# A two-layer diffusion backbone in fp32: stores of normalised tokens issued by GpSimd, and three SwiGLU tiles begun on the first half's tokens

## The chip, the core and the metric

The kernel runs on one core of a Trainium2 chip. TensorE (PE) multiplies, VectorE (DVE), ScalarE (ACT) and GpSimd (POOL) do the elementwise work, and SyncE (SP) issues the DMAs. Each of these engines works through its own queue in order: an instruction that waits holds up everything queued behind it on that engine. The metric is the device time of one execution in microseconds.

## What is computed

Latent and context tokens, 256 of each with 1024 features, go through two layers. Cut to what matters here:

```python
for l in range(2):
    m_x = split(silu(c) @ w_ada[l] + b_ada[l], 9)        # shift, scale, gate: three of each; m_c likewise from c_ctx
    x = post_norm(x, 0.5 * m_x[2] * swiglu(modulate(x, m_x[0], m_x[1]), ffn1_wi[l], ffn1_wo[l]), ln_g[l, 0], ln_b[l, 0])
    # the same for ctx
    y_x, y_c = hybrid_mixer(modulate(x, m_x[3], m_x[4]), ...)   # attention, RWKV, neighbourhood attention
    x = post_norm(x, m_x[5] * y_x, ...)                  # ctx in layer 0 only
    x = post_norm(x, 0.5 * m_x[8] * swiglu(modulate(x, m_x[6], m_x[7]), ...), ...)

def swiglu(u, wi, wo):
    gate, up = split(u @ wi, 2)
    return (silu(gate) * up) @ wo                        # 1024 -> 2 x 2816 -> 1024
def post_norm(x, y, g, b): return layer_norm(ALPHA * x + y, g, b)
```

## The kernel before, in words

Features lie on partitions and tokens on columns. The 512 columns are two halves: latent tokens (0 to 255, the first half) and context tokens (256 to 511, the second half). A product in full precision is three passes: each operand is split into a rounded high part and the rest, by one ACT copy (`whi`, `uh`; lines 320 and 336) and one DVE subtraction (`wlo`, `ul`; lines 321 and 337), and `gemm` (lines 330 to 332) multiplies high by high, low by high and high by low.

`wload` (line 312) loads a weight tile of 128x1024 into `raw`, of which there are three buffers, and splits it into `whi` and `wlo`, of which there are two each. A caller can give other buffers to hold the split tile (`hold`, four pieces of 128x512).

A stage is a SwiGLU (`ffn`) or a mixer. At its end the two halves are normalised one after the other: `ln_stats` sums squares on PE, takes `pow` on POOL (line 428) and spreads the result with a transpose (`ps_bc`). `ln_norm` multiplies (line 440), modulates for the next stage (`modulate`: `u`, `uh`, `ul`), and, in a second loop, has POOL scale the tokens for the residual path (`xn`, line 447), which SP stores to DRAM (`xd<-xn`, line 450). `xn` has two buffers, so the third one waits until the first store has landed. The second half's normalisation runs while PE has only the first half's tokens to work on.

A SwiGLU has 22 tiles m, each with a gate and an up product (`ps_fg`, `ps_fu`; PSUM has six banks for them, three tiles). With two halves, `early` tiles are started on the first half's columns and then finished on the second's; the others take all 512 columns at once. `swiglu` (line 496 and on) makes `sg` from both products and splits it into `hh` and `hl`. Tile 0's weights are loaded ahead (`make_ready`); those of the other early tiles are held in buffers of `hh` and `hl`.

Beside this, the modulations of later stages are worked out in pieces (`ada_pieces`): a piece loads 128x1024 of `w_ada` (`araw`, two buffers, line 242) and adds it to an accumulator with two DVE instructions (lines 251 and 253). `bg_after(1)` takes one piece from the list and queues its DVE instructions behind the latest `wlo` (`self.lo`). There are 45 pieces in the two SwiGLUs of layer 0 and 36 in the first of layer 1; two are taken with each tile.

Three SwiGLUs have two halves: both of layer 0 and the first of layer 1. Five normalisations store with `xn` on POOL: the two of those SwiGLUs that end in a mixer, the one that ends in a SwiGLU, and the two mixers. The last mixer and the last SwiGLU have only the first half.

The mixer begins with four tiles of `w_in`; the weights of two of them are held in buffers called `wG`, and its next tile is split into `phi` and `plo`.

A framework places the instructions: it lays each engine's order down ahead of time from the order in which the program names them, their dependencies and its own estimate of times, and adds waits where a buffer's memory was used by something before.

Of the kernel before, what the change touches and what calls it, by code (L numbers as in the profile page):

```python
# [112 lines left out]
class Program:  # L113
# [320 lines left out]
    def ln_norm(self, l, ln, h, nxt, dst, bc, res=None):  # L434


        nc, z = self.nc, self.z
        for k in range(KD):
            with (self.tc.issue_after(res.ins) if res is not None and k >= 3 else nullcontext()):
                nc.vector.tensor_tensor(out=z[k][:, h], in0=z[k][:, h], in1=bc, op=ALU.mult)  # L440
                if nxt is not None:
                    self.modulate(k, h, z[k][:, h], *nxt)
        for k in range(KD):
            xn = self.tmp.tile([P, SEQ], F32, tag="xn", name="xn", bufs=2 if nxt is not None else 4)
            lg, lb = [self.lng[:, l, ln, i, k:k + 1] for i in range(2)]
            if nxt is not None:
                nc.gpsimd.tensor_scalar(out=xn, in0=z[k][:, h], scalar1=lg, scalar2=lb, op0=ALU.mult, op1=ALU.add)
            else:
                nc.scalar.activation(out=xn, in_=z[k][:, h], func=AF.Identity, scale=lg, bias=lb)
            nc.sync.dma_start(out=dst[k][:, h], in_=xn)  # L450

    def norm_dst(self, l, ln, nxt, final=None):
        if nxt is not None:
# [8 lines left out]
    def ffn(self, l, which, halves, nxt_fn, every, final=None, then=()):  # L462
        nc = self.nc
# [4 lines left out]
        with ExitStack() as ctx:  # L468
# [7 lines left out]
            two = len(halves) == 2  # L476
            slots = iter(range(2 * KF))

            def load(m, held=False):
                ws = []  # L480
                for i in range(2):
                    hold = None
                    if held and m > 0:
                        hold = [[hp.tile([P, NT], F32R, tag=t, name="w" + t) for t in ("hh", "hl")] for _ in range(2)]
                    ws.append(self.wload(wi[m, i], 1024, hold=hold))
                    if next(slots) % every == 0:
                        self.bg_after(1)
                return ws

            def wi_gemm(ps, ws, h):  # L490
                for p, w in zip(ps, ws):
                    self.gemm(p[:, h], w, [t[:, h] for t in self.uh], [t[:, h] for t in self.ul])

            def swiglu(pg, pu):
                sg = self.tmp.tile([P, NT], F32, tag="sg", name="sg")
                nc.scalar.activation(out=sg[:, full], in_=pg[:, full], func=AF.Silu)
                nc.vector.tensor_tensor(out=sg[:, full], in0=pu[:, full], in1=sg[:, full], op=ALU.mult)
                a = hp.tile([P, NT], F32R, tag="hh", name="hh")
                b = hp.tile([P, NT], F32R, tag="hl", name="hl")
                self.split(a[:, full], b[:, full], sg[:, full])  # L500
                hh.append(a)
                hl.append(b)

            def banks():
                return [self.bank("mm", [P, NT], n) for n in ("ps_fg", "ps_fu")]


            early = 2 if two else 0
            ps = [banks() for _ in range(early)]
            ready, self.ready = self.ready, []  # L510
            ws = [m == 0 and ready or load(m, True) for m in range(early)]
            for h in halves if two else []:
                for m in range(early):
                    wi_gemm(ps[m], ws[m], h)
                    if h.start:
                        self.bg_after(1)
            for p in ps:
                swiglu(*p)
            for m in range(early, KF):
                p = banks()  # L520
                wi_gemm(p, m == 0 and ready or load(m), full)
                swiglu(*p)
                if self.bgpe:
                    self.bgpe.pop(0)()
            self.bg_all()
            gate = self.gate(l, gi)
            nxt = nxt_fn()
            dst = self.norm_dst(l, ln, nxt, final)
# [1126 lines left out]
```

## Time and profile before

| | |
|---|---|
| runs, us | 2874.34, 2883.58, 2884.24 |
| median, us | 2883.58 |
| profiled execution, us (its span) | 2877.69 (2875.9) |
| PE busy | 2706.8 us, 94% |
| DVE, ACT, POOL busy | 59%, 39%, 8% |
| mean granted TensorE clock | 0.963 |

"Busy" counts instructions at work. The timeline lists an engine's instructions in order of time, with what they waited for; the table of stretches shows the busy time of each engine between two points and the granted clock of TensorE.

### The profile page before, as it was taken

The numbers are of one execution on the slowest core, as the hardware profiler recorded it, in microseconds if no ns is written. First come the engines' busy times: TensorE is split into PE (matmuls) and PEld (weight loads), VectorE is DVE, ScalarE is ACT, GpSimd is POOL, SyncE is SP. The second block draws the span as 40 slices with busy tenths as digits, with TensorE's granted clock in tenths as the row PEclk, the third lists the DMA queues.
The fourth block names the chain that finished last, engine by engine and source line by source line (L and its number), as shares of the span: only waits on it lengthen the run. The fifth ranks groups of instructions, "written<-read, shape, count | busy, mean of one in ns | idle before, by whom it ended". The sixth has DMA issues, their size and how long they took to land. (4 is left out here: it accounts for less than half of the span.)

```text
span 2875.9 us, 48513 instructions
## 1 busy us (share of the span) xinstructions
PE 2706.8 (94%) x19654; PEld 2202.5 (77%) x19654; DVE 1704.9 (59%) x2855; ACT 1123.3 (39%) x2088; POOL 224.0 (8%) x242
## 2 busy tenths in 40 slices
PE   7999998999899899999999999999899998898998
PEld 5778887676667676787888878888877777777998
DVE  5667345767652457657762477533578775385654
ACT  3222235534432346342222332222565543373543
POOL 0000011000000101220000110001200000122000
PEclk9999998999999999999999999999999989898999
DMA  7655342321223533435553465433342223544654
GB/s 283 205 184 174 106 127 92 86 61 52 57 82 122 156 112 91 141 128 189 178 167 107 125 202 182 140 99 113 121 117 72 70 63 96 167 132 137 221 175 152
DMA packets 207616, 379.75 MB, mean 132 GB/s; under 512 B 80032, under 2 KB 110368, under 8 KB 207392
## 3 DMA queue, kind: packets, MB, share of 16 engines
q1 hardware_dynamic: 207392, 376.65, 42.2%
q8 instruction: 154, 2.52, 0.4%
q14 instruction: 70, 0.57, 0.1%
HBM read 342.50 MB, written 33.03 MB: 131 GB/s over the span
## 5 line engine op out<-in xcount | busy, mean ns | idle before, releaser
L320 ACT ACTIVATE whi<-raw 128x1024 fp32r<-128x1024 f32 (+1 forms) x399 | 415.2, 1041 | 1097.0 <-PE ps_o L331 297.3
L321 DVE TENSOR_TENSOR wlo<-raw,whi 128x1024 fp32r<-128x1024 f32 (+1 forms) x399 | 499.4, 1252 | 497.8 <-ACT whi L320 485.9
L847 PE MATMUL ps_gate<-uh,whi 128*128 128x512 f32 (+1 forms) x672 | 268.0, 399 | 4.6 <-ACT fg L853 3.3
L330 PE MATMUL ps_o<-hh,whi 128*128 128x512 f32 (+1 forms) x770 | 268.8, 349 | 0.0
L253 DVE SCALAR_TENSOR_TENSOR acc<-araw,cs,acc 128x1024 f32<-128x1024 f32 x210 | 260.5, 1279 | 13.6 <-DMA araw<-in_w_ada 13.0
L332 PE MATMUL ps_o<-hh,wlo 128*128 128x512 f32 (+1 forms) x770 | 267.9, 348 | 0.0
L331 PE MATMUL ps_o<-hl,whi 128*128 128x512 f32 (+1 forms) x770 | 266.6, 346 | 0.0
L330 PE MATMUL ps_fg<-uh,whi 128*128 128x512 f32 (+1 forms) x704 | 256.5, 364 | 7.6 <-ACT uh L336 3.8
L332 PE MATMUL ps_fg<-uh,wlo 128*128 128x512 f32 (+1 forms) x704 | 254.5, 361 | 6.7 <-DVE wlo L321 6.7
L332 PE MATMUL ps_fu<-uh,wlo 128*128 128x512 f32 (+1 forms) x704 | 251.9, 358 | 4.7 <-DVE wlo L321 4.7
L331 PE MATMUL ps_fg<-ul,whi 128*128 128x512 f32 (+1 forms) x704 | 253.6, 360 | 0.1
L330 PE MATMUL ps_fu<-uh,whi 128*128 128x512 f32 (+1 forms) x704 | 251.2, 357 | 0.9 <-ACT whi L320 0.9
L331 PE MATMUL ps_fu<-ul,whi 128*128 128x512 f32 (+1 forms) x704 | 250.9, 356 | 0.0
L849 PE MATMUL ps_gate<-uh,wlo 128*128 128x512 f32 (+1 forms) x672 | 243.8, 363 | 1.3 <-DVE wlo L321 1.3
L848 PE MATMUL ps_gate<-ul,whi 128*128 128x512 f32 (+1 forms) x672 | 243.6, 362 | 0.0
L330 PEld LDWEIGHTS ps_fg<-uh,whi 128*128 128x128 f32 x704 | 135.3, 192 | 39.1 <-ACT whi L320 12.0
L847 PEld LDWEIGHTS ps_gate<-uh,whi 128*128 128x128 f32 x672 | 132.4, 197 | 36.7 <-issue 7.2
L330 PEld LDWEIGHTS ps_o<-hh,whi 128*128 128x128 f32 x770 | 144.7, 188 | 20.4 <-ACT whi L320 1.7
L331 PEld LDWEIGHTS ps_o<-hl,whi 128*128 128x128 f32 x770 | 144.5, 188 | 20.1
L332 PEld LDWEIGHTS ps_o<-hh,wlo 128*128 128x128 f32 x770 | 144.7, 188 | 18.2
L332 PEld LDWEIGHTS ps_fg<-uh,wlo 128*128 128x128 f32 x704 | 135.1, 192 | 27.7 <-DVE wlo L321 8.2
L332 PEld LDWEIGHTS ps_fu<-uh,wlo 128*128 128x128 f32 x704 | 133.7, 190 | 26.1 <-DVE wlo L321 7.4
(299 smaller groups left out, 5099.4 us busy)
## 6 DMA issues: line engine op xcount, KB each, us to landing
raw<-in_ffn_wi SPq DMA_DIRECT2D x176, 512.0 KB, 3.6
araw<-in_w_ada SPq DMA_DIRECT2D x144, 512.0 KB, 3.8
raw<-in_w_in SPq DMA_DIRECT2D x92, 512.0 KB, 3.6
raw<-in_ffn_wo SPq DMA_DIRECT2D x70, 448.0 KB, 3.3
raw<-in_ffn_wo SPq DMA_DIRECT2D x35, 512.0 KB, 3.5
pd<-fg SPq DMA_DIRECT2D x52, 256.0 KB, 2.1
raw<-in_w_branch SPq DMA_DIRECT2D x24, 512.0 KB, 4.0
raw<-in_w_in SPq DMA_DIRECT2D x44, 256.0 KB, 2.7
```

The lines of the kernel that those rows point to most:

```text
L253: nc.vector.scalar_tensor_tensor(out=a, in0=raw, scalar=c, in1=a, op0=ALU.mult, op1=ALU.add)
L320: nc.scalar.activation(out=hi[:, :m], in_=r, func=AF.Copy)
L321: self.lo = nc.vector.tensor_tensor(out=lo[:, :m], in0=r, in1=hi[:, :m].bitcast(F32), op=ALU.subtract)
L330: nc.tensor.matmul(pt, wh, xh[k], start=first and k == 0, stop=False)
L331: nc.tensor.matmul(pt, wh, xl[k], start=False, stop=False)
L332: nc.tensor.matmul(pt, wl, xh[k], start=False, stop=last and k == n - 1)
L847: nc.tensor.matmul(pt, wh, xh, start=k == 0, stop=False)
L848: nc.tensor.matmul(pt, wh, xl, start=False, stop=False)
L849: nc.tensor.matmul(pt, wl, xh, start=False, stop=k == KD - 1)
```

## The change

GpSimd instead of SP issues the store of `xn` wherever a next stage follows. In a SwiGLU with two halves three tiles instead of two begin on the first half. The pieces that were taken with the held weight tiles and with the second half's products are no longer taken there; two are taken behind each early tile's `swiglu`. So six pieces are named by the end of tile 2, as before, and two with each later tile, as before. Since `self.lo` is then the last split of tile 2, all six are queued behind that on DVE.

```diff
-            nc.sync.dma_start(out=dst[k][:, h], in_=xn)
+            (nc.sync if nxt is None else nc.gpsimd).dma_start(out=dst[k][:, h], in_=xn)
...
-                    if next(slots) % every == 0:
+                    if not held and next(slots) % every == 0:
                         self.bg_after(1)
...
-            early = 2 if two else 0
+            early = 3 if two else 0
             ps = [banks() for _ in range(early)]
             ready, self.ready = self.ready, []
             ws = [m == 0 and ready or load(m, True) for m in range(early)]
             for h in halves if two else []:
                 for m in range(early):
                     wi_gemm(ps[m], ws[m], h)
-                    if h.start:
-                        self.bg_after(1)
             for p in ps:
                 swiglu(*p)
+                self.bg_after(2)
```

## Rows read from the trace of the kernel before

**Rows 1.** Stretches, busy us (instructions) per engine, then granted clock, DMA share, GB/s

```profile
425.00:458.00 33.00, 24.11 (x140) 21.26 (x139) 18.32 (x46) 19.23 (x45) 11.24 (x15) 0.75 0.47 140
1240.00:1312.00 72.00, 65.58 (x414) 57.33 (x415) 50.46 (x82) 30.86 (x60) 14.21 (x19) 0.95 0.50 163
1312.00:1625.00 313.00, 313.00 (x1429) 255.98 (x1428) 174.26 (x186) 82.37 (x100) 13.62 (x12) 1.00 0.48 151
```

**Rows 2.** The store's line and its tile: ns min/median/max; landing; us

```profile
L447 POOL TENSOR_SCALAR xn<-z,c_lngb x72: 553/557/2562, 422.0 to 2667.1; 128x256 f32<-128x256 f32 x72
L450 SPq DMA_DIRECT2D xd<-xn x72: 319/320/1594, 422.6 to 2667.7; - x72
DMA to landing us min/median/max: 1.7/1.7/4.7
```

**Rows 3.** First mixer's start: timeline (start, us, instruction [idle before <-releaser]) and a stretch

```profile
427.21 1.22 DVE L321 TENSOR_TENSOR wlo<-raw,whi 128x1024 fp32r<-128x1024 f32 x1
431.88 0.36 SPq L602 DMA_DIRECT2D raw<-in_w_in  x1
435.62 0.63 ACT L336 ACTIVATE phi<-raw 128x512 fp32r<-128x512 f32 x1 [3.15 <-DMA raw<-in_w_in]
436.61 2.72 PE L424 MATMUL ps_ss<-ones,sq 128*128 128x1 f32 x12 [1.78 <-ACT sq L420]
441.68 1.09 POOL L447 TENSOR_SCALAR xn<-z,c_lngb 128x256 f32<-128x256 f32 x2 [1.37 <-DVE z L440]
455.89 1.67 ACT L320 ACTIVATE wG<-raw 128x512 fp32r<-128x512 f32 x3 [2.96 <-DMA xd<-xn]
456.57 0.58 PE L330 MATMUL ps_first<-uh,wG 128*128 128x256 f32 x1 [2.43 <-ACT wG L320]
436.60:439.30 2.70, 2.69 (x12) 2.63 (x12) 0.38 (x1) 0.57 (x2) 0.00 (x0) 0.50 0.27 97
```

**Rows 4.** Timeline, second mixer's start

```profile
2041.72 1.97 PE L424 MATMUL ps_ss<-ones,sq 128*128 128x1 f32 x12 [2.04 <-ACT sq L420]
2043.97 0.70 POOL L428 TENSOR_TENSOR rs<-rs,mhalf 128x2 f32<-128x2 f32 x1 [6.16 <-DVE rs L427]
2046.04 1.09 POOL L447 TENSOR_SCALAR xn<-z,c_lngb 128x256 f32<-128x256 f32 x2 [1.37 <-DVE z L440]
2058.71 1.67 ACT L320 ACTIVATE wG<-raw 128x512 fp32r<-128x512 f32 x3 [1.46 <-DVE sh L897]
```

**Rows 5.** Second SwiGLU's start: timeline, a stretch, SP's wait, the load's median landing

```profile
1261.06 1.09 ACT L351 ACTIVATE u<-z,mb,mg 128x256 f32<-128x256 f32 x2 [4.74 <-DVE z L440]
1261.19 1.09 POOL L447 TENSOR_SCALAR xn<-z,c_lngb 128x256 f32<-128x256 f32 x2 [1.11 <-DVE z L440]
1275.79 0.81 SPq L242 DMA_DIRECT2D araw<-in_w_ada  x2
SPq L242 <- DMA xd<-xn: 0.9, 2, 0.6
araw<-in_w_ada SPq DMA_DIRECT2D x144, 512.0 KB, 3.8
1286.45 5.05 DVE L253 SCALAR_TENSOR_TENSOR acc<-araw,cs,acc 128x1024 f32<-128x1024 f32 x4
1292.69 0.80 PE L332 MATMUL ps_fg<-uh,wlo 128*128 128x512 f32 x1 [4.06 <-DVE wlo L321]
1293.00:1301.00 8.00, 7.92 (x23) 5.87 (x22) 7.66 (x7) 0.51 (x1) 0.00 (x0) 0.66 0.74 244
```

**Rows 6.** Timeline of PE, third SwiGLU's start

```profile
1645.18 0.38 PE L330 MATMUL ps_fg<-uh,whi 128*128 128x256 f32 x1 [1.47 <-ACT uh L336]
1685.15 0.50 PE L332 MATMUL ps_fg<-uh,wlo 128*128 128x512 f32 x1 [1.16 <-DVE wlo L321]
```

**Rows 7.** Timeline, last SwiGLU's start

```profile
2658.10 1.09 POOL L447 TENSOR_SCALAR xn<-z,c_lngb 128x256 f32<-128x256 f32 x2 [1.37 <-DVE z L440]
2669.65 1.28 ACT L496 ACT_TABLE_LOAD   x1 [0.92 <-DVE wlo L321]
```

## The prediction, made before the changed kernel was run

> **What bounds the kernel now.** I read the table of stretches first, to see where PE isn't at work. Inside a SwiGLU it never stops: 313.00 us busy of 313. Where one stage hands over to the next it does: 24.11 of 33 us at the first mixer's start with a granted clock of 0.75, 65.58 of 72 around the second SwiGLU's [rows 1]. The change touches only these seams, so all that it can give or cost is there: the first SwiGLU's start, then five seams in which tokens are normalised and stored. Next I read PE's timeline in each seam for the waits, then the timeline of the engine that each wait names, then the queue of SP.
>
> At the mixers' starts PE waits for squares from ACT, 1.78 and 2.04 us [rows 3, 4]. ACT was held by `phi`, which waited 3.15 us for a weight load that SP issued at 431.88 [rows 3], behind stores that wait for POOL. A `raw` buffer had come free when `wlo` ended, 427.21 + 1.22 = 428.43 [rows 3]; so 3.4 us of the load's delay are SP's queue. Later PE waits 2.43 us for `wG`, and `wG` waits for the landing of the last store, since it takes over memory [rows 3].
>
> At the second SwiGLU's start PE stands 4.06 us for a `wlo` on which DVE comes late: modulation pieces stand ahead of it in DVE's queue [rows 5]. Those began late because their loads were issued only at 1275.79, behind the stores, and waited for the landing of a store too [rows 5]. At the third SwiGLU's start a wait of 1.47 us goes back to a weight load behind stores, and three more, of 1.16, 0.95 and 1.02 (the first is shown), are `wlo` behind pieces [rows 6].
>
> **Part 1, the stores.** 72 of 0.32 us leave SP, 23 us of issuing that no end depends on [rows 2]. What counts is that weight loads no longer stand behind stores that wait for POOL. The squares' waits go: 1.78 and 2.04. In the first, the twelve `ps_ss` matmuls behind it took 2.72 us at a granted clock of 0.50, the lower level; at the higher they take 1.36, so 1.4 more, and 0.6 at the second mixer, where the same twelve took 1.97 [rows 3, 4]. I count both, with zero as the other end, since the normalisation's own pause behind them stays and can lower the clock a little later. At the third SwiGLU I let 1.1 of the 1.47 go, three quarters, since the load's own landing stays; ends zero and all of it [rows 6].
>
> The price is on POOL. Call c what issuing one store costs it. The trace has no DMA from POOL, so I bound c by the shortest and the longest issue on SP, 0.32 and 1.59 us [rows 2]. A POOL instruction with two columns to work on takes 0.70 [rows 4]; that plus one issue of 0.32 is 1.0, which I take, because it is the row of POOL itself with the least work in it. Below zero c can't go: POOL issues nothing now. A pair of buffers then turns in the longer of 2 x (0.56 + c) and 0.56 + c + 1.7 (landing) [rows 2]: 3.26 us at c = 1.0, and eight stores take 3 x 3.26 + 2 x 1.56 + 1.7 = 14.6 us from the first `xn` to the last landing (11.2 at c = 0.32, 19.0 at 1.59). What they take now: 455.89 - 441.68 = 14.2 at the first mixer, 12.7 at the second, 14.6 at the second SwiGLU (1275.79 - 1261.19), and at most 11.6 at the last, whose table load at 2669.65 didn't wait for it any more [rows 3, 4, 5, 7]. Who waits for that: `wG` at both mixers (+0.4 and +1.9 on the path), and the first `sg` of a SwiGLU, with ACT's next `whi` behind it. At the last SwiGLU the table load ahead of `sg` moves from 2669.65 to 2658.10 + 14.6 = 2672.7 [rows 7], 3.0 us, and the next tile's `whi` behind it; PE has a tile of work left then, so the cost is between 0 and 3.0, and I take 2.0, nearer to the upper end because nothing else hides a late `whi`. Also queued on POOL behind a store is `pow` of the second half; at c = 1.0 the first half's eight stores end before it is due, so nothing.
>
> The page "DMA: Bandwidth & Descriptors" of the Trainium skill (section Latency and other measured facts) speaks against this part: first byte about 1 us from GpSimd and 0.6 from SP, because software writes the descriptors. By it each of four turns would be about 0.4 us longer, an estimate of 1.6 us more at both mixers and the last SwiGLU, some 5 us in all; no row here shows a store from GpSimd.
>
> **Part 2, the third tile.** No PE work is added: 48 matmuls on 256 columns twice, instead of 48 on 512. Its weights are split in eight pieces instead of four instructions, during the normalisation, where ACT idles 4.74 us ahead of the second half's `u` [rows 5]; uncovered it would be 0.6 us a SwiGLU. PE has no pause between the first half's two tiles and the second half's, so a third adds nothing there. What it buys is at tile 3: `whi` and `wlo` come free when tile 0 is done, with 10.5 us of PE work on tiles 1 and 2 still to go (96 matmuls of half the 0.22 us that one takes on average in the long stretch [rows 1]), so tile 3's splits can lie ahead of the pieces. At the very first SwiGLU both halves are ready and I count nothing.
>
> **Part 3, the pieces.** As many as before, in the same total; their loads still wait for the stores' landing (`araw` takes over memory of theirs, as SP's wait shows [rows 5]). So POOL's pace, not SP's queue, sets when they begin, about as now at c = 1.0. They no longer stand ahead of tile 3's `wlo`, but can stand ahead of tile 4's: the first piece lands at 1275.79 + 3.8 = 1279.6, and PE, which stood at 1288.6 near the start of a tile, gets to tile 4 about 10.5 us later, at 1299.1 [rows 5]; in these 19.5 us DVE has six `sg` and `hl` (half a `wlo` of 1.22 each, 3.7 [rows 3]), one `wlo` and pieces of 2.5 (half of 5.05 us for four instructions [rows 5]). Five fit, a sixth makes PE wait, and a seventh and eighth are named with tile 3. I leave 1.5 us of wait where 4.06 was: -2.6. The stretch behind that wait had the clock at 0.66 for 7.92 us of work [rows 5], so (1 - 0.66) x 7.92 = 2.7 us go with it, if the wait is short; a wait of 1.16 us at the third SwiGLU is followed by full clock. There I take half of the three waits' 3.1: -1.5. Ends: all of both gone, or none.
>
> **Sum**, in us: first mixer -1.8 - 1.4 + 0.4 = -2.8; second SwiGLU -2.6 - 2.7 = -5.3; third -1.1 - 1.5 = -2.6; second mixer -2.0 - 0.6 + 1.9 = -0.7; last SwiGLU +2.0; total -9.4. Against the profiled execution's 2877.69 us (its span is 2875.9) that is 2868; this execution lies 6 us below the median of 2883.58, and I forecast the median: 2874 us, 0.3% less.
>
> **The rivals.** (a) *POOL is cheap and the waits vanish.* c near 0.32: the landing comes 3.0 and 1.5 us sooner at the mixers, the last SwiGLU loses nothing, pieces begin 3.4 us sooner and no `wlo` waits: -6.2, -4.1, -6.8, -4.2, 0 = -21, so 2862. For it: every wait goes back to SP's queue or the stores. Against: POOL's `pow` on two columns alone takes 0.70. 27 in 100.
>
> (b) *The wait only moves.* Pieces that begin at 1280 or later stand ahead of tile 4's `wlo` as they now do ahead of tile 3's, at the same cost; with the rest of the sum -2.8 - 1.1 - 0.7 + 2.0 = -2.6, so 2881. For it: the number of pieces by tile 2 is the same, and their loads stay bound to the landing. 20 in 100.
>
> (c) *Stores from POOL are slow.* c at 1.59: the stores take 19.0 us. `wG` comes 4.8 and 6.3 us later, `sg` of the last SwiGLU 7.4 with a wait of 6; `pow` of the second half stands behind the first half's stores (8 x 2.15 = 17 us) by 1 to 2 us at four seams, 5 in all; the SwiGLUs give nothing. So -5.8 of squares and clock, -1.1, + 4.8 + 6.3 + 6 + 5 = +15, and with the pieces later too up to +25: near 2900. It decides from c of about 1.5. 13 in 100. The page "SBUF — State Buffer" of the Trainium skill (section SBUF: two separate sides) has a mechanism for it: DVE instructions that take both SBUF ports lock GpSimd out of writing descriptors; no run so far shows it.
>
> **How the numbers follow.** The forecast has 40 in 100, (a) 27, (b) 20, (c) 13. A measurement of this kernel can tell about 0.5%, 14 us, from no change: below 2869 is (a), 0.27; within, the forecast and (b), 0.60; above, (c), 0.13. The range takes in (b), nearly all of (a) and half of (c): 2857 to 2899.
>
> **What would show it.** Right: a store issue on POOL near 1.0 us; no wait for `sq` behind `phi` at either mixer; the wait for `wG` still there and released by the store; DVE with tile 3's `wlo` ahead of the pieces. Wrong: PE waits of over 3 us at tile 4, POOL's `pow` late, or stores that land over 16 us after the first `xn`.

## The result, and the profile of the changed kernel

The changed kernel takes 2895.4 us (median of 6 runs, 2890.3 to 2898.8); the kernel before, run beside it, 2876.1 us (6 runs, 2871.6 to 2884.2). The ratio is 1.0057, with a 95% interval of 1.0043 to 1.0072: **the change makes the kernel 0.6% slower**, by some 16 to 19 us. 2874 us was predicted, 0.3% below the 2883.58 us known then, with 2899 as the upper end of the range and 13 in 100 for slower. The time lies inside the range, but the kernel moved the other way. The profiled execution took 2894.86 us; its span is 2893.1 us, against 2875.9 before.

The store is now a GpSimd instruction. These are two groups of POOL in the changed kernel (line, engine, operation, tiles, shape, count | total busy time in us, mean ns of one | total idle time before them in us and what ended it):

```profile
L447 POOL TENSOR_SCALAR xn<-z,c_lngb 128x256 f32<-128x256 f32 x72 | 54.6, 758 | 30.1 <-DVE z L440 11.6 <-DMA xd<-xn 9.4 <-DVE z L418 4.2
L450 POOL DMA_DIRECT2D xd<-xn x72 | 42.7, 593 | 21.4 <-POOL xn L447 19.6 <-DMA xd<-xn 1.8
```

The store among its DMA issues (queue, count, KB each, median us to landing):

```profile
xd<-xn POOLq DMA_DIRECT2D x72, 128.0 KB, 2.1
```

And the same normalisation among the groups of the kernel before:

```profile
L447 POOL TENSOR_SCALAR xn<-z,c_lngb 128x256 f32<-128x256 f32 x72 | 54.0, 756 | 59.2 <-DMA xd<-xn 29.4 <-DVE z L440 19.4 <-DVE ul L337 5.0
```

Issuing a store takes POOL 0.59 us, and 0.30 us pass ahead of it (19.6 / 66 by the tile's view): 0.89 us of POOL for one store. It lands after 2.1 us, where SP's landed after 1.7 [rows 2]. The normalisation itself is not slower than before (758 ns and 756), but its mean is 0.76 us, not the 0.56 us of the median row [rows 2].

POOL's timeline ahead of the last SwiGLU shows one turn after another (start, us, instruction, idle before it):

```profile
2666.56 0.56 POOL L447 TENSOR_SCALAR xn<-z,c_lngb 128x256 f32<-128x256 f32 x1 [1.38 <-DVE z L440]
2667.41 0.62 POOL L450 DMA_DIRECT2D xd<-xn  x1 [0.30 <-POOL xn L447]
2668.09 0.95 POOL L447 TENSOR_SCALAR xn<-z,c_lngb 128x256 f32<-128x256 f32 x1
2669.34 0.59 POOL L450 DMA_DIRECT2D xd<-xn  x1 [0.30 <-POOL xn L447]
2669.97 1.08 POOL L447 TENSOR_SCALAR xn<-z,c_lngb 128x256 f32<-128x256 f32 x1
...
2680.93 0.59 POOL L450 DMA_DIRECT2D xd<-xn  x1 [0.30 <-POOL xn L447]
```

Here two buffers no longer buy any overlap: POOL is busy with the turn itself, 1.93 us on average (these eight normalisations have a mean of 0.93 us), and no turn waits for a landing. At the mixers' starts one turn in eight waits 1.1 to 1.2 us for one, at the second SwiGLU's three wait 2.3 us together. What waits for the last of the eight stores is ACT, and behind ACT stands PE (their timelines, changed kernel):

```profile
2683.28 1.28 ACT L496 ACT_TABLE_LOAD   x1 [5.92 <-DMA xd<-xn]
2685.12 1.06 ACT L320 ACTIVATE whi<-raw 128x1024 fp32r<-128x1024 f32 x1
2686.23 0.58 PE L330 MATMUL ps_fg<-uh,whi 128*128 128x256 f32 x1 [2.98 <-ACT whi L320]
```

Two stretches behind that wait (length, busy us and instructions per engine, granted clock, DMA share, GB/s):

```profile
2686.20:2690.00 3.80, 3.31 (x13) 3.02 (x14) 3.79 (x6) 1.64 (x3) 0.00 (x0) 0.51 0.91 319
2690.00:2695.50 5.50, 5.50 (x36) 5.50 (x36) 2.88 (x4) 1.33 (x2) 0.00 (x0) 0.72 0.63 233
```

The table load came at 2669.65 before and did not wait for a store [rows 7]; now it waits 5.92 us, 16.7 us after the first `xn`. PE stands 2.98 us, and then works for some 9 us at a mean granted clock of 0.51 and then 0.72 of its higher level, which costs about as much as the standing: (1 - 0.51) x 3.31 + (1 - 0.72) x 5.50 = 3.2 us.

At the starts of the mixers one wait went and two grew (timelines of ACT, POOL and PE at the first mixer, changed kernel):

```profile
435.05 0.64 ACT L336 ACTIVATE phi<-raw 128x512 fp32r<-128x512 f32 x1 [0.63 <-DMA raw<-in_w_in]
441.19 0.59 POOL L450 DMA_DIRECT2D xd<-xn  x1 [0.30 <-POOL xn L447]
441.81 0.73 POOL L428 TENSOR_TENSOR rs<-rs,mhalf 128x2 f32<-128x2 f32 x1
442.60 0.69 PE L431 MATMUL ps_bc<-c_ident,rs 128*128 128x128 f32 x2 [3.17 <-POOL rs L428]
460.32 0.63 ACT L320 ACTIVATE wG<-raw 128x512 fp32r<-128x512 f32 x1 [5.27 <-DMA xd<-xn]
461.12 0.55 PE L330 MATMUL ps_first<-uh,wG 128*128 128x256 f32 x1 [3.88 <-ACT wG L320]
```

PE's wait for `pow` in the kernel before:

```profile
440.37 0.69 PE L431 MATMUL ps_bc<-c_ident,rs 128*128 128x128 f32 x2 [1.04 <-POOL rs L428]
```

`phi` waits 0.63 us for its load instead of 3.15, and no PE wait for squares is left at either mixer [rows 3, 4]. But `pow` (L428) now starts at 441.81 right behind the first half's last store, and PE waits for it: 3.17 us, where the kernel before had 1.04, and 2.31 us at the second mixer. `wG` is released by the landing 5.27 us late, and PE waits 3.88 us for it instead of 2.43 [rows 3]; at the second mixer 3.81, where the kernel before had 0.65.

In the second and third SwiGLU the wait is at tile 4 (PE's timeline in the changed kernel; `ps_ada` are the matmuls that close a modulation):

```profile
1310.92 0.79 PE L332 MATMUL ps_fg<-uh,wlo 128*128 128x512 f32 x1 [3.25 <-DVE wlo L321]
1316.53 0.64 PE L258 MATMUL ps_ada<-acc,one 128*32 128x512 f32 x4 [1.81 <-issue]
1702.63 0.50 PE L332 MATMUL ps_fg<-uh,wlo 128*128 128x512 f32 x1 [3.05 <-DVE wlo L321]
1708.11 1.08 PE L258 MATMUL ps_ada<-acc,one 128*32 128x512 f32 x4 [3.45 <-DVE acc L253]
```

Against 4.06 us [rows 5] and 1.16, 0.95 and 1.02 us [rows 6]: the waits for `wlo` moved by a tile, and with those at the closing matmuls they became no shorter. The wait of 1.47 us at the third SwiGLU's start [rows 6] is gone, and so is every wait of over 0.3 us at tile 3.

### The profile page after: what moved, and what is told of

The parts are those of the page before. It is cut to its first block, busy times and chain, and to the rows that moved or that the text cites. A ratio compares the mean times of both kernels' runs of the same rounds, so it can differ in the third digit from the quotient of the medians.

```text
span 2893.1 us, 48830 instructions
## 1 busy us (share of the span) xinstructions
PE 2714.3 (94%) x19798; PEld 2215.0 (77%) x19798; DVE 1706.0 (59%) x2861; ACT 1122.5 (39%) x2094; POOL 269.2 (9%) x314
## 4 chain that ended last, share of the span: by engine, by line
PE 50%; DVE 6%; DMA 3%; issue 3%; ACT 2%; POOL 2%; SPq 0%; POOLq 0%; ACTq 0%; DVEq 0%
PE ps_o L330 3%; PE ps_o L332 3%; PE ps_o L331 3%; PE ps_fu L332 3%; PE ps_fg L332 3%; PE ps_fg L330 3%; PE ps_fg L331 3%; PE ps_fu L331 3%; PE ps_fu L330 3%; PE ps_gate L846 2%; PE ps_o L663 2%; PE ps_gate L847 2%; PE ps_gate L848 2%; PE ps_t L655 1%; PE ps_s L640 1%
## 5 line engine op out<-in xcount | busy, mean ns | idle before, releaser
L320 ACT ACTIVATE whi<-raw 128x1024 fp32r<-128x1024 f32 (+1 forms) x393 | 408.8, 1040 | 1073.5 <-PE ps_o L331 297.3
L321 DVE TENSOR_TENSOR wlo<-raw,whi 128x1024 fp32r<-128x1024 f32 (+1 forms) x393 | 491.6, 1251 | 499.0 <-ACT whi L320 493.0
L253 DVE SCALAR_TENSOR_TENSOR acc<-araw,cs,acc 128x1024 f32<-128x1024 f32 x210 | 260.9, 1279 | 16.8 <-DMA araw<-in_w_ada 16.5
L330 PE MATMUL ps_fg<-uh,whi 128*128 128x512 f32 (+1 forms) x680 | 248.0, 365 | 8.4 <-ACT whi L320 6.0
L332 PE MATMUL ps_fg<-uh,wlo 128*128 128x512 f32 (+1 forms) x680 | 246.5, 362 | 7.2 <-DVE wlo L321 7.2
L331 PE MATMUL ps_fg<-ul,whi 128*128 128x512 f32 (+1 forms) x680 | 245.5, 361 | 0.1
L332 PE MATMUL ps_fu<-uh,wlo 128*128 128x512 f32 (+1 forms) x680 | 242.2, 356 | 3.1 <-DVE wlo L321 3.1
L330 PE MATMUL ps_fu<-uh,whi 128*128 128x512 f32 (+1 forms) x680 | 241.4, 355 | 0.4 <-ACT whi L320 0.4
L331 PE MATMUL ps_fu<-ul,whi 128*128 128x512 f32 (+1 forms) x680 | 241.4, 355 | 0.0
L848 PEld LDWEIGHTS ps_gate<-uh,wlo 128*128 128x128 f32 x672 | 132.4, 197 | 20.9 <-DVE wlo L321 2.0
```

The costliest lines, as they stand in the source:

```text
L253: nc.vector.scalar_tensor_tensor(out=a, in0=raw, scalar=c, in1=a, op0=ALU.mult, op1=ALU.add)
L320: nc.scalar.activation(out=hi[:, :m], in_=r, func=AF.Copy)
L321: self.lo = nc.vector.tensor_tensor(out=lo[:, :m], in0=r, in1=hi[:, :m].bitcast(F32), op=ALU.subtract)
L330: nc.tensor.matmul(pt, wh, xh[k], start=first and k == 0, stop=False)
L331: nc.tensor.matmul(pt, wh, xl[k], start=False, stop=False)
L332: nc.tensor.matmul(pt, wl, xh[k], start=False, stop=last and k == n - 1)
```

## The experiments

Every kernel was timed beside the kernel before on the same chip, 6 to 12 runs of each, so the ratios can be set side by side. The change has three parts: who issues the stores, how many early tiles there are, and when the pieces come. "Late" below is the change's order (pieces only behind the early tiles' SwiGLUs), "early" that of the kernel before, "later" a third order (no piece before the first full tile's loads).

| stores issued by | early tiles | pieces | ratio to before | 95% interval |
|---|---|---|---|---|
| SP (kernel before again) | 2 | early | 0.9988 | 0.9972 to 1.0004 |
| POOL | 2 | early | 1.0023 | 1.0009 to 1.0038 |
| POOL for first halves, SP else | 2 | early | 0.9977 | 0.9962 to 0.9993 |
| SP for first halves, POOL else | 2 | early | 1.0061 | 1.0039 to 1.0082 |
| SP | 3 | early | 1.0007 | 0.9994 to 1.0019 |
| SP | 2 | late | 0.9968 | 0.9956 to 0.9980 |
| SP | 3 | late | 1.0013 | 0.9997 to 1.0029 |
| POOL | 2 | late | 1.0022 | 1.0007 to 1.0037 |
| POOL (the change) | 3 | late | 1.0057 | 1.0043 to 1.0072 |
| POOL for first halves, SP else | 2 | late | 0.9964 | 0.9944 to 0.9984 |
| POOL for first halves, SP else | 3 | late | 0.9997 | 0.9979 to 1.0016 |
| SP | 2 | later | 0.9973 | 0.9950 to 0.9995 |
| SP | 3 | later | 1.0006 | 0.9987 to 1.0025 |
| POOL for first halves, SP else | 2 | later | 0.9943 | 0.9922 to 0.9965 |

### The same program twice

> The kernel before, unchanged, as a second kernel: a ratio within 0.1% of 1, and a second profile of the same program. It tells which differences of a stage between two profiles are only two executions. If the wait of 4.06 us at the second SwiGLU, the 2.43 us at the first wG and the absence of a wait in the last SwiGLU are there again to 0.5 us, then the waits belong to the program; stretches inside the mixers may then still differ by 2 to 4 us, with PE's granted clock.

Measured: 0.9988 (0.9972 to 1.0004). So two sets of runs of one program can differ by about 0.1%, and single ratios nearer to 1 than that say nothing. PE's wait at the second SwiGLU, in PE's timeline of this second profile:

```profile
1296.26 0.50 PE L332 MATMUL ps_fg<-uh,wlo 128*128 128x512 f32 x1 [1.54 <-DVE wlo L321]
```

It is 1.54 us where the first profile had 4.06 [rows 5], and 3.20 us in a kernel further down that is edited only far from this seam (eight tiles in halves). `wG` at the first mixer has 2.43 again, at the second 2.00 for 0.65, and the last SwiGLU has no wait again. The expectation was wrong for the one wait on which the largest term of the prediction's sum stands: that size belonged to one execution.

### The stores

All stores from GpSimd and nothing else:

```diff
-            nc.sync.dma_start(out=dst[k][:, h], in_=xn)
+            (nc.sync if nxt is None else nc.gpsimd).dma_start(out=dst[k][:, h], in_=xn)
```

> The kernel before with one edit: the stores of normalised tokens are issued by GpSimd; early tiles and pieces stay as before. Theory A (the stores are the cost): a turn of GpSimd is 1.93 us for one row (normalisation, 0.30 us of gap, 0.59 us of issue) and the landing 2.1 us later, so the eight stores of a half land 16.4 to 17.5 us after the first normalisation, and gates that take over that memory or read those tokens wait: +1.4 us at the first mixer's wG and about +2 at its pow, +2.6 at the second mixer, +3.3 and +3.5 in the last SwiGLU, 13 to 20 us in all, 2889 to 2896 us beside 2876, with the waits for DMA at wG and sg as long as in the changed kernel (5.3 us, 4.6 us, 5.9 us on ACT). Theory B (the third tile and the late pieces are the cost, because the wait for weights comes back at tile 4 with 3.1 to 3.5 us in two SwiGLUs): this kernel has neither, so within 5 us of the kernel before. Theory C (both, about half each): 2884 to 2888 us.

Measured: 1.0023, 2887 us beside 2880, some 7 us. That is less than theory A's 13 to 20 us, and between theory B's 5 at most and theory C's 8 to 12 (2884 to 2888 beside 2876): this run alone doesn't decide between B and C. The waits are theory A's, though: 3.81 us at `wG`, 3.01 us in the last SwiGLU.

One half's stores each: `nc.gpsimd if nxt is not None and res is not None else nc.sync` for the first halves (32 stores), and `res is None` for the other 40:

> The kernel before with GpSimd issuing only the stores of the first of two halves (the other half, and norms that are not in two halves, on SyncE). If theory A's late landing of the last eight stores is what costs, this kernel has nothing of it: within 4 us of the kernel before, its last stores landing 11 to 14.6 us after the first normalisation as before. If what costs is GpSimd's and SyncE's queues as a whole (all 72 stores), it has half of the loss of the kernel with all stores on GpSimd, +6 to +10 us.

> The kernel before with GpSimd issuing only the stores of the second of two halves and of norms in one piece. By theory A (late landing of the last eight stores) nearly the whole loss of the kernel with all stores on GpSimd is here, +10 to +18 us, with the same waits at wG and sg; by a cost of each store wherever it stands, about half of it; by theory B, none.

Measured: 0.9977 and 1.0061. **The two halves of this part work against each other.** The first half's stores on GpSimd give 0.2%, though the interval reaches that of the same program twice: the squares' waits are gone at both mixers (though PE then waits 2.48 us for `pow` instead of 1.04), SP is free, and no gate of the next stage (`wG`, `sg`) waits for these landings. The second half's cost 0.6%: what comes next waits for them. With all stores on GpSimd both act, and the sum, 0.4%, agrees with 1.0023 within the intervals. Four pairs in the table differ only in the second halves' stores; they cost 0.46 to 0.61% in each. Four differ only in the first halves' and have SP for the others; they gain 0.04 to 0.30%.

Which part of a store from GpSimd makes the last landing late, the time on POOL or the way to memory? In the next kernel SP issues all stores again, and POOL normalises twice in the second half:

```diff
-                nc.gpsimd.tensor_scalar(out=xn, in0=z[k][:, h], scalar1=lg, scalar2=lb, op0=ALU.mult, op1=ALU.add)
+                for _ in range(2 if res is None else 1):
+                    nc.gpsimd.tensor_scalar(out=xn, in0=z[k][:, h], scalar1=lg, scalar2=lb, op0=ALU.mult, op1=ALU.add)
```

> The kernel before with one edit: in the second of two halves (and in norms in one piece) GpSimd does each normalisation twice, into the same tile; stores stay on SyncE. It lengthens GpSimd's turn by 0.56 to 1.0 us, about the 0.89 us that issuing a store there takes, and leaves the landing as it is. Theory A1 (GpSimd's turn per row is what makes the last landing late): the eight stores land 15.5 to 17.5 us after the first normalisation, wG waits 3.5 to 4 us at both mixers, PE waits 2 to 3.4 us in the last SwiGLU, and the time is 10 to 18 us over the kernel before, as with the second half's stores on GpSimd. Theory A2 (the longer way of a store from GpSimd to its landing, 2.1 us for 1.7, and what it holds on the DMA's side is what makes it late): at most a third of that.

Measured: 1.0038 (1.0023 to 1.0054), 11 to 12 us, theory A1's size with no store on GpSimd, where the second half's stores cost 1.0061. PE's wait in its last SwiGLU:

```profile
2680.03 0.39 PE L330 MATMUL ps_fg<-uh,whi 128*128 128x256 f32 x1 [2.71 <-ACT whi L320]
```

The `wG` waits are 2.99 and 3.18 us, less than the 3.5 to 4 expected. So a longer turn of POOL is enough for most of the loss, and the timeline of the last SwiGLU above says the same: no turn waits for a landing there, so the longer way, 2.1 us for 1.7, enters once, behind the last store. What is left between 1.0038 and 1.0061 is not clear of the intervals.

The changed kernel with the stores of the last norm alone given back, and with those of all second halves given back (`(l, ln) == (1, 1)`, and `res is None`, on `nc.sync`):

> The changed kernel with one part undone: the last of the stored norms, ahead of the last SwiGLU, is stored by SyncE again; the other 64 stores stay on GpSimd. Theory L (the last SwiGLU's start takes 6 to 8 us of the loss: PE's wait for whi of 2.98 us and the lower clock behind it): that wait gone, the last SwiGLU's stage 213 to 215 us instead of 219.5, the whole 5 to 8 us below the changed kernel, 1.003 to 1.004 of the kernel before. Rival (the loss is spread over all seams alike): 2 us or less.

> The changed kernel with one part undone: the second half's stores go back to SyncE; the first half's stay on GpSimd, three early tiles and late pieces stay. Theory A: the waits for wG and in the last SwiGLU are gone (below 2.5 us at wG, none of 2.98 us in the last SwiGLU), and the time is 12 to 20 us below the changed kernel, 0.998 to 1.001 of the kernel before. Rival (the parts of the change harm each other whatever half is stored from where): less than 6 us below the changed kernel, 1.003 or more.

Measured: 1.0030 and 0.9997, that is 0.27% (some 8 us) and 0.60% (some 17 us) below the changed kernel. Theory L and theory A hold. The stage of the last SwiGLU, from its norm to the next norm, as a stretch with the columns above, in the kernel before:

```profile
2646.17:2859.63 213.46, 204.11 (x1637) 199.24 (x1636) 128.51 (x163) 94.14 (x137) 9.73 (x15) 0.97 0.58 185
```

The changed kernel:

```profile
2654.80:2874.29 219.49, 207.34 (x1636) 201.96 (x1635) 128.65 (x163) 93.82 (x137) 17.33 (x23) 0.95 0.56 180
```

The one that normalises twice:

```profile
2647.21:2867.13 219.92, 207.66 (x1636) 202.19 (x1635) 128.50 (x163) 94.10 (x137) 17.71 (x23) 0.95 0.57 180
```

The one with the last norm's stores back on SP:

```profile
2657.14:2870.41 213.27, 204.31 (x1636) 199.24 (x1635) 128.74 (x163) 94.03 (x137) 10.40 (x15) 0.97 0.59 186
```

With the same matmuls the late landing makes this stage 6.0 to 6.5 us longer, and PE's own busy time is 3.2 to 3.6 us of that: the clock behind the wait (0.95 for 0.97 over the stage). By the ratios the last SwiGLU is nearly half of what the second halves' stores cost, with 6 to 7 us of uncertainty in each difference of ratios; by the stage it is 6.2 us. Of the rest the profiles show 4 us at the first mixer's start (125.2 us without, 129.2 with them, the first part of the mixer as below); in the second SwiGLU they show none (392.8 and 392.7).

### The tiles and the pieces

The change without its first part, and each of the other two alone (`early = 3`; and two early tiles with `bg_after(2)` behind each early tile's SwiGLU):

> The changed kernel with one edit: the stores go back to SyncE; three early tiles and the late pieces stay. Theory A: the waits at wG and in the last SwiGLU are again those of the kernel before (2.43 us, 0.65 us, none), the second SwiGLU keeps what the third tile gave, and the whole is 2868 to 2877 us. Theory B: the waits at tile 4 stay (3.25 us in the second SwiGLU, 3.05 and 3.45 us in the third), and the whole is 2884 to 2896 us. Theory C: 2880 to 2886 us. A wait that stays at tile 4 with the time near that of the kernel before would say that tile 4's wait only replaces the earlier one.

> The kernel before with one edit: three early tiles instead of two; the pieces stay where they were (one behind each early tile of the second half, so three instead of two), stores from SyncE. Theory 1 (the late pieces make the new wait at tile 4, as two are issued behind every tile's splits): here the wait at tile 4 is below 1.5 us and the kernel is 3 to 8 us faster than the kernel with tiles and late pieces, 2872 to 2878. Theory 2 (the wait belongs to the third tile: tile 3's and tile 4's weights are asked of ACT and DVE in one go behind three SwiGLUs): the wait at tile 4 is 2.5 us or more as there, and the time within 3 us of it.

> The kernel before with one edit: the pieces of the next modulation come only behind the early tiles' SwiGLUs, two behind each; two early tiles, stores from SyncE. Theory 1 (the pieces are what delays the splits): the wait of 4.06 us at tile 3 is gone or below 1 us, and one at tile 4 of 2 to 4 us takes its place; the time is within 4 us of the kernel before. Theory 2 (the wait is the third tile's own matter): no wait of over 1.5 us at either tile, and the time 4 to 6 us below the kernel before.

Measured: 1.0013, 1.0007 and 0.9968. The first is not clear of no change; a wait of 2.63 us stays at tile 4 of the second SwiGLU, so there, as the first text's last sentence has it, the later wait only replaces the earlier one, whoever stores. The late pieces alone are a gain of 0.3%, and the third tile takes all of it back. With two tiles and late pieces PE waits 1.29 us at tile 3 (PE's timeline, second SwiGLU) and 1.55 us at the closing matmuls:

```profile
1300.33 0.50 PE L332 MATMUL ps_fg<-uh,wlo 128*128 128x512 f32 x1 [1.29 <-DVE wlo L321]
```

That is nearest to theory 2, with more time than it gave: no wait of the old size is left, and no third tile was needed for that. But the kernel before had only 1.54 us there in its second profile, so the gain stands by the times, and where it arises isn't shown. Nor does it hold beside all stores from GpSimd: two tiles take 1.0023 there with early pieces and 1.0022 with late ones. With three tiles and early pieces the `wlo` wait is gone, but the closing matmuls stand in PE's queue for the last piece, in the second and in the third SwiGLU (PE's timeline):

```profile
1307.48 1.06 PE L258 MATMUL ps_ada<-acc,one 128*32 128x512 f32 x8 [3.08 <-issue]
1701.39 1.93 PE L258 MATMUL ps_ada<-acc,one 128*32 128x512 f32 x8 [5.49 <-DVE acc L253]
```

This is the kernel in which the first of the two theories hoped for 3 to 8 us less than with late pieces; by the ratios it took 2 us less.

Then both numbers of tiles with pieces still later (`self.bg_after(2)` behind the early tiles taken out):

> Three early tiles, stores from SyncE, and no piece behind the early tiles at all: the first comes with tile 3's loads, one with each load from there. Theory 1 (the third tile does what was forecast, and only the pieces that stand ahead of tile 4's splits bring the wait back): no wait of over 1.5 us at tiles 3 and 4 of the second and third SwiGLU, and 4 to 10 us below the kernel with three tiles and late pieces (1.0013), 0.997 to 1.000. Theory 2 (what waits is the closing matmuls of a modulation, which stand in TensorE's queue until the last piece has been added up on VectorE, wherever the pieces begin): a wait of 2 to 5 us for ps_ada stays, only at a later tile, and the time within 3 us of 1.0013.

> The same with two early tiles: stores from SyncE, no piece behind the early tiles, the first with tile 2's loads. Beside the run with three tiles it gives what the third tile is worth where the pieces come later. By the forecast the third tile gives time: this kernel 2 to 5 us slower than that one. By the runs so far (two tiles 0.9968, three 1.0013, both with late pieces) it takes time: this kernel 5 to 13 us faster than that one. Both within 3 us: the third tile is worth nothing by itself.

Measured: 1.0006 and 0.9973. In both the waits at tiles 3 and 4 and at the first closing matmuls are gone, so theory 1 of the first text had the waits right and not the time: the time is 2 us from 1.0013, theory 2's size, without theory 2's wait, and three tiles are again 0.33% slower than two. The second SwiGLU's stage as a stretch, with three tiles:

```profile
1238.68:1628.81 390.13, 386.29 (x1962) 323.58 (x1961) 229.25 (x280) 115.62 (x169) 30.52 (x33) 1.00 0.49 152
```

With two:

```profile
1233.10:1620.32 387.22, 384.15 (x1915) 320.11 (x1914) 228.22 (x278) 116.12 (x167) 28.99 (x33) 1.00 0.51 153
```

Three tiles take 2.9 us more, 2.1 of them PE's busy time, at full clock. That two early tiles would be the faster ones by 5 to 13 us was the expectation by the runs so far; it holds (9.7 us). So a tile in halves seems to be more work. To price that alone, tiles 8 to 15 of the kernel before, far from any seam, were multiplied half by half:

```diff
-                wi_gemm(p, m == 0 and ready or load(m), full)
+                w = m == 0 and ready or load(m)
+                for h in halves if two and 8 <= m < 16 else [full]:
+                    wi_gemm(p, w, h)
```

> The kernel before with one edit: in the three SwiGLUs over both halves, tiles 8 to 15, far from any seam, are multiplied half by half (96 matmuls of 256 columns a tile instead of 48 of 512). It prices a tile in halves alone. By the traces (24 matmuls of 256 columns start every 2.83 us, 24 of 512 every 5.44) a tile in halves takes 4 x 2.83 = 11.3 us against 10.9, so 0.43 us each, 24 tiles, +10 us: 1.0035 of the kernel before. If the third tile's whole cost of 9 to 13 us in three SwiGLUs were TensorE's work (3 to 4 us a tile), it would be +70 to +100 us. By the prediction (no work added): none.

Measured: 1.0051 (1.0036 to 1.0067), 14.7 us for 24 tiles, 0.6 us each. One such tile as a stretch:

```profile
1366.85:1378.37 11.52, 11.52 (x98) 11.52 (x97) 7.28 (x8) 3.24 (x4) 0.00 (x0) 1.00 0.36 126
```

One whole tile of the kernel before:

```profile
1325.30:1336.18 10.88, 10.88 (x49) 9.01 (x48) 8.53 (x8) 3.20 (x4) 0.00 (x0) 1.00 0.57 194
```

It takes 11.52 us against 10.88; PEld, the weight loads, is busy all the time with 256 columns a load, and 9.01 of 10.88 us with 512. A third tile therefore costs 1.3 to 2 us in three SwiGLUs by its halves. That is a fifth of the 10 us or so (0.33 to 0.45%) between two and three tiles. The traces show a little more: the waits for `wlo` and at the closing matmuls in the second and third SwiGLU come to 7.3 us with three tiles and late pieces and to 6.2 with two (those of 0.5 us and more). The rest, some 7 us, is not located: in the four pairs of profiles the stages of the second and third SwiGLU together are 5.3, 7.8 and 3.7 us longer with three tiles and once 2.6 us shorter. By the intervals each difference between two ratios is uncertain by 6 to 9 us, but all four have the same sign and nearly the same size.

The changed kernel with two early tiles instead of three:

> The changed kernel with one part undone: two early tiles instead of three; all stores from GpSimd and late pieces stay. Theory T (the third tile costs by itself, 0.3 to 0.45% as in the pairs with stores from SyncE): 9 to 13 us below the changed kernel, 1.000 to 1.003. Rival (with stores from GpSimd the pieces begin later anyway, so that the third tile is neutral or needed there): within 4 us of the changed kernel, or above it.

Measured: 1.0022, 0.35% below the changed kernel. Theory T holds: within the intervals the third tile costs the same whoever stores.

### A kernel that is faster than both

> Two parts of the change, each of which alone came out below the kernel before: GpSimd issues the stores of the first of two halves only (alone 0.9977), and the pieces come only behind the early tiles' SwiGLUs, with two early tiles (alone 0.9968). Theory A (the harm is in the second half's stores and in the third tile; the rest of the change is good): the two add up, 0.9935 to 0.9965 of the kernel before, no wait for squares at either mixer, and none in the last SwiGLU. Rival (one of the two small gains, or both, was only the spread of executions, as the unchanged kernel against itself gave 0.9988): 0.997 to 1.001.

Measured: 0.9964 (0.9944 to 0.9984), at the upper edge of what theory A gave, with no wait for squares and none in the last SwiGLU; the rival's lower end is as near, so it doesn't decide. With the pieces still later:

> GpSimd issues the first half's stores only, two early tiles, and no piece before tile 2's loads. If the two gains (0.9977 alone; 0.9973 for the pieces) add up: 0.994 to 0.996 of the kernel before, no wait for squares at the mixers, and none of over 1 us at tiles 3 and 4 of the SwiGLUs. If they don't: 0.996 to 0.998, as the run with late pieces and the first half's stores gave (0.9964).

Measured: **0.9943 (0.9922 to 0.9965), 2859.9 us, some 16 us less than the kernel before**; this lies at the sum of its parts (0.9977 and 0.9973 give 0.9950). It has 6 runs. Three stages as stretches, the first part of the first mixer, the second and the third SwiGLU (the second number is the length), in the kernel before:

```profile
410.16:539.34 129.18, 117.95 (x791) 97.14 (x789) 82.98 (x178) 70.91 (x140) 16.55 (x23) 0.92 0.33 101
1230.29:1624.81 394.52, 387.65 (x1914) 321.78 (x1913) 228.56 (x278) 115.85 (x167) 29.27 (x33) 0.99 0.48 150
1624.81:2015.11 390.30, 383.17 (x1873) 317.94 (x1872) 214.19 (x265) 117.80 (x169) 28.87 (x30) 1.00 0.46 147
```

Its second profile:

```profile
413.39:542.51 129.12, 118.10 (x790) 97.30 (x789) 82.99 (x178) 71.05 (x140) 16.36 (x23) 0.92 0.34 101
1233.74:1625.82 392.08, 387.77 (x1915) 322.51 (x1913) 228.61 (x278) 116.08 (x167) 27.00 (x33) 0.99 0.49 151
1625.82:2016.47 390.65, 383.95 (x1873) 319.23 (x1872) 213.98 (x265) 118.11 (x169) 27.93 (x30) 0.99 0.48 147
```

The changed kernel:

```profile
413.33:542.51 129.18, 115.20 (x790) 94.49 (x788) 83.69 (x178) 70.61 (x140) 24.50 (x39) 0.95 0.32 101
1239.00:1631.67 392.67, 386.39 (x1962) 323.34 (x1961) 229.40 (x280) 115.72 (x169) 39.47 (x49) 1.00 0.48 151
1631.67:2025.05 393.38, 385.06 (x1920) 321.51 (x1919) 213.98 (x267) 117.60 (x171) 37.32 (x46) 0.98 0.46 146
```

This one:

```profile
411.91:535.59 123.68, 114.22 (x790) 93.46 (x789) 83.64 (x178) 70.82 (x140) 18.34 (x31) 0.96 0.36 105
1227.15:1616.38 389.23, 386.02 (x1914) 321.77 (x1913) 229.47 (x278) 116.00 (x167) 35.34 (x41) 1.00 0.49 152
1616.38:1999.59 383.21, 381.28 (x1872) 317.58 (x1871) 213.70 (x264) 117.71 (x169) 31.73 (x38) 1.00 0.48 150
```

The three stages together: 914.0, 911.9, 915.2 and 896.1 us. What the prediction hoped to gain in these seams, some 11 us, was there to be had, and more, as far as one profile of each can say; the changed kernel gets none of it.

The table adds the change up: its gainful half (first halves' stores and late pieces with two tiles) is 0.36% faster, the third tile then costs 0.33%, and the second halves' stores 0.60%, which makes 1.0057.

## Why the prediction was wrong, point by point

**In short.** Part 1 gave eight stores 14.6 us and charged 0.4, 1.9 and 2.0 us for them; they took 16.5 to 17.5 us, and giving the second halves' stores back to SP saves 0.60%, some 17 us. Part 2 gave the third tile no cost; going back to two tiles saves 0.35%, some 10 us. Each of these is more than the whole gain forecast, 9.4 us.

**The cost of an issue was right, the turn was not.** c was taken as 1.0 us; the runs show 0.30 + 0.59 = 0.89. But the turn was built with a normalisation of 0.56 us, the median of its row [rows 2], and eight turns need the mean, 0.76 us over all 72, and 0.77 to 0.93 in the four groups of eight that count here: in the last SwiGLU one takes 0.95 to 1.08 us while DVE has `ul` splits, and 0.55 to 0.56 otherwise, but for one of 1.59 beside `wlo`. In the kernel before the mean is the same. With two buffers and a landing of 2.1 us the eight stores took 16.5, 16.5, 17.5 and 16.7 us from the first `xn` to the release at the first mixer, the second mixer, the second and the last SwiGLU; 14.6 was forecast for all four.

**The last SwiGLU cost three times what was written for it.** The right chain was named (landing, table load, `whi`), and 2.0 us written for it; it is 6.0 in the stage, and over all kernels here 6.0 to 8.3 where the last stores land late, 1.2 at most where they don't. Two sizes failed: the landing came 2.1 us later than forecast, and the clock behind PE's wait was left out. The sum gave the clock back wherever a wait was to go (1.4, 0.6 and 2.7 us) and charged nothing where one was to come. Here PE's busy time grew by 3.2 us.

**`wG` and `pow`.** The wait for `wG` stayed, as forecast, and grew by 1.4 us at the first mixer (0.4 forecast), and from 0.65 to 3.81 us at the second (1.9 more forecast), where the landing had not been what `wG` waited for [rows 4], so that the 12.7 us taken for its stores were only an upper bound. `pow` was said to be free at c = 1.0, since the first half's stores would be done; they were not, and it costs PE 2.1 and 1.3 us more. This took back what the squares' waits gave, 1.78 and 2.04 us; those did go, for the stated reason.

**The second SwiGLU** was to give 5.3 us, the largest term. It rested on one execution's wait of 4.06 us with its low clock; the same program's second profile has 1.54 us. Against that one the changed kernel has no gain in this stage at all (392.67 and 392.08 us). Tile 3's splits did come ahead of the pieces, as forecast. But the pieces' loads were issued 17.5 us after the first `xn` and not 14.6, and 1.5 us of wait was left at tile 4 where 3.25 came; with all stores on SP it is still 2.63. So rival (b) took place as described: pieces stand ahead of tile 4's `wlo` (3.25 and 3.05 us), with one thing more that the prediction did not see: the matmuls that close a modulation stand in PE's own queue and stop it until DVE has the last piece (1.81 and 3.45 us).

**The third tile** was said to add no work to PE. It does, 0.6 us each, and by the pairs of runs it costs 0.33 to 0.45% beside late or later pieces whoever stores. The late pieces, which were only thought of as its companion, are the part of the change that gains most (0.9968 alone, but nothing beside all stores from GpSimd).

**The rivals.** (c), 13 in 100, is what the second half's stores did, by way of `wG` and `sg` as it says; `pow` is late behind the first half's (PE waits 2.48 us for it at the first mixer with those alone on GpSimd, 1.04 with the second half's alone). But it was to decide only from c of about 1.5, and with c at 0.89 the turn was long enough. (b), 20 in 100, is what the SwiGLUs did. They were given as cases that exclude each other, and both came. (a) could not have paid what it says: it takes 3.0 and 1.5 us off waits for `wG` that were 2.43 and 0.65 us. What the prediction listed as signs that it was wrong, waits of over 3 us at tile 4, a late `pow`, and stores landing over 16 us after the first `xn`, are all three in the trace. On the page "DMA: Bandwidth & Descriptors" of the Trainium skill (section Latency and other measured facts): its 0.4 us more for a store from GpSimd is what the trace shows from issue to landing (2.1 and 1.7 us). The estimate of about 1.6 us a seam made with it had the right direction by luck: it puts 0.4 us on each of four turns, and in the last SwiGLU no turn waits for a landing. The lock named by the page "SBUF — State Buffer" of the Trainium skill (section SBUF: two separate sides) was not seen in the issues, which took 587 to 742 ns with a mean of 593; whether any DVE instruction beside them takes both ports, no run here shows.

**What stays open.** Between the two profiles compared first, the first mixer behind its first part is 5.5 us longer after the change (691.0 and 696.5 us), with no operation of the change in it. Over all kernels here this stage lies between 689 and 697 us, with no pattern by part: 689.2 and 696.8 us both have all stores on GpSimd. It is counted as the spread of single executions, not as an effect. With it, two thirds of the 17.2 us between the two profiles lie outside the seams for which the sum has a term: 3.2 us ahead of the first mixer (as much as between two profiles of the kernel before), 5.5 here, and 2.5 behind the last SwiGLU. In the seams' stages, in the order of the sum, -2.8, -5.3, -2.6, -0.7 and +2.0 us were forecast, and 0.0, -1.9, +3.1, -1.3 and +6.0 us measured. So the parts' costs rest on the ratios of many runs, and of the profiles only the last SwiGLU's stage repeats in every kernel. Some 7 us of the third tile's cost are not located either.

## What to carry to other kernels

Before a DMA is moved to another engine, ask for each transfer who waits for its landing: the first half's stores had hardly anyone waiting and did no harm, the second half's had the next stage's first instructions behind them and lost. Build a pace from means, not medians, and price a wait that comes with the clock behind it, as you do a wait that goes. A single profile's wait is one draw: take a second one before a term of several us is rested on it.

## What the runs showed of the hardware

A store of 128 KB that POOL issues costs it 0.59 us and 0.30 us ahead of it, and lands 2.1 us after its issue; from SP the issue is 0.32 us and the landing 1.7 [rows 2]. Twice as many matmuls of 256 columns for the same sum are not free: a tile takes 11.52 us instead of 10.88, with PEld busy throughout. The granted clock also differs between profiles where no part of the change is at work: in the kernel with only the first halves' stores on GpSimd, PE ran a stretch ahead of the second SwiGLU, with no wait in it, at 0.72, where the kernel before has 1.00 (columns as above):

```profile
1236.00:1254.40 18.40, 18.40 (x117) 18.13 (x118) 6.06 (x14) 4.47 (x12) 6.87 (x10) 0.72 0.12 37
```

Between the two sets of matmuls for the mean that bound this stretch (`ps_mean`, one for each half), 21.3 us pass there and 17.2 in the kernel before, and 18.7 in the same program's second profile. That is up to 4 us in a stage, about the size of several terms of the sum.
